# A compact tile for the diagonal blocks of chunked linear attention, and an entry stage that scales by a diagonal product

## The chip, the cores and the metric

The kernel runs on one core of a Trainium2 chip. The metric is the time of one execution in device microseconds, the median of three runs. A core has five engines with a queue of instructions each: TensorE (PE; its weight loads are listed as PEld), VectorE (DVE), ScalarE (ACT), GpSimd (POOL) and SyncE (SP, which here only issues DMAs). An instruction starts when it is at the head of its engine's queue and the semaphores that it waits for are set.

## What is computed

One layer of an encoder on x of 1024 tokens by 1024 channels: a norm, three token mixers side by side (HGRN2, GLA, a gated delta rule), gates, an output product, and a squared-ReLU MLP. The change touches the first norm and the two mixers that are gated linear attention:

```python
h = rmsnorm(x, ln_mix_pre)            # x * rsqrt(mean(x^2) + eps) * w
# gated_linear_attention, per head; f = exp(log_f) per token and key channel
# S_t = diag(f_t) S_{t-1} + k_t v_t^T ;  o_t = S_t^T q_t
# within a chunk: a[i, j] = sum_k q[i, k] * prod_{j < m <= i} f[m, k] * k[j, k]   (j <= i)
# o = a @ v + (q decayed) @ S
```

HGRN2 has 8 heads with values of 128 channels, GLA 4 heads with 256: 12 heads in all.

## The kernel before

A tile scheduler sets the order of the instructions on each engine from a written order of parts (`ORDER`, near line 930), from priorities (`high_priority` with an offset moves instructions ahead) and from its own estimate of durations. The large projections of the normed input with the weights (`product`, line 195; each weight and each activation is split into a high and a low part, and three products are summed) are by far the most of PE's work. The scheduler puts such products between the small matmuls of the mixers, so that PE has something to do while another engine prepares the next small step.

**The entry stage** (`stage_in`): x comes in eight tiles of 128 tokens by 1024 channels, four buffers, two at a time. `front` squares a tile on ACT with a sum, takes the root (`rstd`: a Sqrt on ACT and small DVE steps) and multiplies the tile by it on DVE (line 292). `back` transposes it in blocks of 128 by 128 on PE (line 302, the second operand is the identity) into PSUM banks of four blocks; from there ACT writes the high part `hT_hi` (line 305) and DVE the low part `hT_lo` (line 306). The first projection (`first_project`) follows pair by pair. Two small Exp calls on ACT belong to other parts: line 262 in `lower_bound` and line 380 in `small_part`. Exp and Sqrt lie in different function tables of ACT, and a change of table is an instruction of its own (ACT_TABLE_LOAD).

**Linear attention** (`linear_attention`, one call a head): the 1024 tokens are 8 chunks of 128. The matrix `at` of a chunk (128 keys on the partitions by 128 queries) is built by doubling: at level h, pairs of neighbouring blocks of h tokens are joined, the second half of the queries against the first half of the keys, with q, k already multiplied by the decay inside their blocks. `update(h)` does the multiplying on DVE: q (line 568), k (line 569) and the block decay f (line 570). Up to blocks of 32 the matmuls are of 32 by 32 quadrants: for each chunk c and each quadrant start s in 0, 32, 64, 96 one small product, lines 576 (level 0, bank `E`), 599 (levels 1 and 2 together, bank `L12`, two banks of four chunks) and 611 (h = 4, 8, 16). `put` copies the entries that a level owns from PSUM into `at` with a mask (COPY_PREDICATED, line 561), once for each quadrant s, since in `at` the four quadrants of a chunk lie in different columns. Levels 32 and 64 are plain copies on ACT into `at` (lines 620 and 625, after the matmuls of lines 617 and 624). Then k is transposed (line 631), the state products (line 640) and the attention products that read `at` (line 643) run, and the state is carried from chunk to chunk on DVE (line 649). `at` is cleared at the start by a memset on POOL (line 549).

In a level's sequence each engine waits for the other: the matmuls of the next level read the q and k that `update` has just written, and `update` may not write before the matmuls of its own level have read.

Of the kernel before, what the change touches and what calls it, by code (L numbers as in the profile page):

```python
# [18 lines left out]
P = 128  # L19
# [43 lines left out]
def layout(inputs):  # L63
# [21 lines left out]
    for n, h in enumerate(LEVELS[2:]):  # L85
# [22 lines left out]
        "conv": np.ascontiguousarray(f["gdn_conv"][0].reshape(4, 24, P).transpose(2, 1, 0)),  # L108
        "alog": rows(f["gdn_a_log"][0]),
        "dtb": rows(f["gdn_dt_bias"][0]),  # L110
        "masks": masks,
        "consts": consts,
    }

# [117 lines left out]
def load_consts(p):  # L232
    nc, c, a = p.nc, p.const, p.a
    cs = c.tile([P, 5, P], F32, name="cs")
    nc.sync.dma_start(cs, a["consts"])
    p.ident, p.tri, p.neg, p.ones = (cs[:, i, :] for i in range(4))
    p.fold = cs[:, 4, 0:64]
    p.lnpre = c.tile([P, 8], F32, name="lnpre")
    nc.sync.dma_start(p.lnpre, a["lnpre"])


def load_more(p):
    nc, c, a = p.nc, p.const, p.a
    mk = c.tile([P, 6, 64], F32, name="mk")
    nc.sync.dma_start(mk, a["masks"])
    p.masks = mk.bitcast(I32)
    for n, w in (("onorm", 512), ("lbl", 8), ("bgk", 4), ("alog", 8), ("dtb", 8)):
        t = c.tile([P, w], F32, name=n)
        nc.sync.dma_start(t, a[n])
        setattr(p, n, t)  # L250
    p.conv = c.tile([P, 24, 4], F32, name="conv")
    nc.sync.dma_start(p.conv, a["conv"])
    nc.vector.tensor_scalar(p.onorm, p.onorm, 0.5, None, ALU.mult)


def lower_bound(p):
# [5 lines left out]
    nc.scalar.activation(e, e, AF.Exp)  # L262
    v.reciprocal(mx, e)
    v.tensor_tensor(e, e, mx, ALU.mult)
    v.tensor_tensor(lb, e, e, ALU.subtract)
    v.tensor_scalar(lb, lb, 0.0, 1.0, ALU.max, ALU.min)
    v.tensor_scalar(om, lb, -1.0, 1.0, ALU.mult, ALU.add)
    p.lb, p.om = lb, om


def stage_in(p):

    nc, v = p.nc, p.nc.vector
    hi = p.hp.tile([P, NK, T], F32R, name="hT_hi", tag="hi")
    lo = p.hp.tile([P, NK, T], F32R, name="hT_lo", tag="lo")
    p.h = (hi, lo)

    def front(t):
        xs = []
        for j in range(2):  # L280
            xt = p.stage.tile([P, D], F32, name=p.name("x_in"), tag="x_in", bufs=4)
            with p.tc.high_priority(offset=p.ahead + 100 if t == 0 else 0):
                nc.sync.dma_start(xt, p.a["x"][(t + j) * P:(t + j + 1) * P, :])
            xs.append(xt)
        if t == 0:
            with p.tc.high_priority(offset=p.ahead + 100):
                load_consts(p)
        for xt in xs:
            junk, ms = p.stage.tile([P, D], F32, name=p.name("junk"), tag="junk"), p.tiny("ms_x", 1)
            nc.scalar.activation(junk, xt, AF.Square, scale=D ** -0.5, accum_out=ms)  # L290
            r = p.rstd(ms, p.eps)
            v.tensor_scalar(xt, xt, r, None, ALU.mult)
        return xs

    def back(t, xs):
        dst = slice(t * P, (t + 2) * P)
        for k0 in range(0, NK, 2):
            b = p.bank("xT")
            for i in range(2):
                for j in range(2):  # L300
                    o = (2 * i + j) * P
                    nc.tensor.transpose(b[:, o:o + P], xs[j][:, (k0 + i) * P:(k0 + i + 1) * P], p.ident)
            for i in range(2):
                k, s = k0 + i, b[:, 2 * i * P:2 * (i + 1) * P]
                nc.scalar.activation(hi[:, k, dst], s, AF.Identity, scale=p.lnpre[:, k:k + 1])  # L305
# [25 lines left out]
def bc(ap, shape):  # L331
    return ap.broadcast_to(list(shape))


def small_part(p):
# [41 lines left out]
    la = p.tiny("la", 64)  # L377
    u, t1 = p.tiny("sp_u", 64), p.tiny("sp_t", 64)
    ea = p.tiny("ea", 8)
    act.activation(ea, p.alog, AF.Exp)  # L380
    u3 = u.rearrange("p (h c) -> p h c", h=8)
    v.tensor_tensor(u3, cab[:, :, 0, :].rearrange("p c h -> p h c"), bc(p.dtb.unsqueeze(2), [P, 8, 8]), ALU.add)
    act.activation(t1, u, AF.Abs)
# [158 lines left out]
def linear_attention(p, q, qx, k, f, v_at, dv, o_out, ss_out):  # L542
# [8 lines left out]
    k3 = k.rearrange("p (c i) -> p c i", c=8)  # L551
    q3 = q.rearrange("p (c i) -> p c i", c=8)

    def put(lev, h, data, c=slice(0, 8)):
        dst = at.rearrange("p (c n two h) -> p c n two h", c=8, two=2, h=h)
        dst = dst[:, c, :, 0 if lev == 0 else 1, :]
        w = 16 // h
        for s in range(0, P, 32):
            n, e = slice(s // 32 * w, s // 32 * w + w), slice(s // 2, s // 2 + 16)
            mask = p.masks[s:s + 32, lev, e].rearrange("p (n h) -> p n h", h=h).unsqueeze(1)  # L560
            v.copy_predicated(dst[s:s + 32, :, n, :], bc(mask, [32, c.stop - c.start, w, h]),
                              data[s:s + 32, :, e].rearrange("p c (n h) -> p c n h", h=h))

    def update(h):
        fb, qb, kb = blocks(f, h), blocks(q, h), blocks(k, h)
# [6 lines left out]
    b = p.bank("E").rearrange("p (c i) -> p c i", c=8)  # L572
    quads = range(0, P, 32)
    for c in range(8):
        for s in quads:
            mm(b[s:s + 32, c, s // 2:s // 2 + 16], k3[:, c, s:s + 32], q3[:, c, s:s + 32:2], start=True, stop=True)
    e = b
# [12 lines left out]
    put(0, 1, e[:, :, 0:64])  # L590
    pairs = []
    for c0 in (0, 4):
        b = p.bank("L12").rearrange("p (c i) -> p c i", c=4)
        for j in range(4):
            c = c0 + j
            q2c = qx[:, c * P:(c + 1) * P].rearrange("p (s i) -> p s i", s=2)
            b2 = b[:, j, :].rearrange("p (s i) -> p s i", s=2)
            for s in quads:
                mm(b2[s:s + 32, :, s // 2:s // 2 + 16], k3[:, c, s:s + 32], q2c[:, :, s // 2:s // 2 + 16], start=True, stop=True)
        pairs.append((b, slice(c0, c0 + 4)))  # L600
    update(2)
    for b, c in pairs:
        put(1, 1, b[:, :, 0:64], c)
        put(2, 2, b[:, :, 64:128], c)
    for lev, h in ((3, 4), (4, 8), (5, 16)):
        b = p.bank("L").rearrange("p (c i) -> p c i", c=8)
        qb = q.rearrange("p (c n two h) -> p c n two h", c=8, two=2, h=h)
        for c in range(8):
            for s in quads:
                n = slice(s // (2 * h), (s + 32) // (2 * h))  # L610
                mm(b[s:s + 32, c, s // 2:s // 2 + 16], k3[:, c, s:s + 32], qb[:, c, n, 1, :], start=True, stop=True)
        update(h)
        put(lev, h, b[:, :, 0:64])
    b = p.bank("L32").rearrange("p (c i) -> p c i", c=8)
    for c in range(8):
        for s in (0, 64):
# [956 lines left out]
```

## Time and profile before

| | us |
|---|---|
| median of 3 runs (2445.07 to 2454.31) | 2445.74 |
| the profiled execution, its own time | 2446.99 |
| its span in the trace | 2445.2 |
| PE busy | 2366.8 |
| DVE busy | 1477.2 |
| ACT busy | 929.1 |
| POOL busy | 86.0 |

A row of the page or of the trace names the engine, the line, the operation and the tiles it writes and reads ("out<-in"), the shape, and in brackets how long the engine stood idle before it and what ended the wait. Matmuls are pipelined: the time beside a matmul is from its start to its modelled end, and the next one starts sooner. In an fp32 product each matmul of the program is recorded as two instructions.

### The profile page before, as it was taken

To read this page: it belongs to the slowest core of one execution; us is meant where nothing else is said; L and a number is where in the kernel's file an instruction comes from. 1 tells how busy PE (TensorE), PEld (TensorE's weight loads), DVE (VectorE), ACT (ScalarE), POOL (GpSimd) and SP (SyncE) were. 2 spreads that over 40 slices of the span, in tenths; PEclk is the share of its full clock that TensorE was granted. 3 is DMA by queue.
4 is the path that set the end of the run, shared out by engine and by line. 5 is a ranking of instruction groups with operands and counts; after the bars stand their busy time and mean duration, and the time that the engine had idled before them with its cause. 6 is when DMAs were issued, how large, how long until landed. Compare 5 with 4: busy or idle time off the path is not lost. (4 is left out here: it accounts for less than half of the span.)

```text
span 2445.2 us, 46222 instructions
## 1 busy us (share of the span) xinstructions
PE 2366.8 (97%) x18782; PEld 2060.4 (84%) x18782; DVE 1477.2 (60%) x3187; ACT 929.1 (38%) x1920; POOL 86.0 (4%) x160
## 2 busy tenths in 40 slices
PE   7999989999999999999999999999999999999998
PEld 6778878988977988889898889998877888788886
DVE  5284599955655446654446654445658655557577
ACT  6863424132323222222221332232434655544453
POOL 0000000000000000000000000000001211100000
PEclk9999999999999999999999999999999999999999
DMA  4455612142221222112221202233333444575454
GB/s 146 138 188 148 192 54 95 36 152 71 66 66 36 72 85 66 49 36 74 87 74 54 70 28 80 57 109 115 115 124 113 168 143 142 181 228 187 153 160 155
DMA packets 166071, 263.64 MB, mean 108 GB/s; under 512 B 42833, under 2 KB 80977, under 8 KB 165729
## 3 DMA queue, kind: packets, MB, share of 16 engines
q1 hardware_dynamic: 145248, 208.23, 27.6%
q0 software_dynamic: 10240, 33.56, 3.8%
q10 hardware_dynamic: 10368, 18.88, 2.1%
q8 instruction: 148, 2.42, 0.4%
q14 instruction: 67, 0.54, 0.1%
HBM read 190.29 MB, written 70.32 MB: 107 GB/s over the span
## 5 line engine op out<-in xcount | busy, mean ns | idle before, releaser
L195 PE MATMUL pj<-whi,hT_hi 128*128 128x256 f32 (+1 forms) x2048 | 581.1, 284 | 6.1 <-ACT hT_hi L305 5.7
L195 PE MATMUL pj<-whi,hT_lo 128*128 128x256 f32 (+1 forms) x2048 | 580.5, 284 | 0.0
L195 PE MATMUL pj<-wlo,hT_hi 128*128 128x256 f32 (+1 forms) x2048 | 579.7, 283 | 0.0
L195 PEld LDWEIGHTS pj<-whi,hT_hi 128*128 128x128 f32 x2048 | 388.2, 190 | 8.6 <-ACT hT_hi L305 6.5
L195 PEld LDWEIGHTS pj<-wlo,hT_hi 128*128 128x128 f32 x2048 | 387.9, 190 | 1.0
L195 PEld LDWEIGHTS pj<-whi,hT_lo 128*128 128x128 f32 x2048 | 387.0, 189 | 1.3 <-issue 0.4
L195 PE MATMUL pj<-hT_hi,whi 128*128 128x512 f32 x768 | 310.7, 405 | 0.0
L195 PE MATMUL pj<-hT_hi,wlo 128*128 128x512 f32 x768 | 309.7, 403 | 0.0
L195 PE MATMUL pj<-hT_lo,whi 128*128 128x512 f32 x768 | 307.7, 401 | 0.0
L168 DVE TENSOR_TENSOR wlo<-wraw,whi 128x1024 fp32r<-128x1024 f32 (+2 forms) x122 | 147.8, 1212 | 158.5 <-ACT whi L168 118.0
L168 ACT CAST whi<-wraw 128x1024 fp32r<-128x1024 f32 (+2 forms) x122 | 126.7, 1039 | 168.9 <-DMA wraw<-in_w_dram 107.2
L195 PE MATMUL ps<-whi,whi 128*128 128x512 f32 x448 | 175.1, 391 | 2.6 <-ACT whi L168 2.4
L195 PE MATMUL ps<-wlo,whi 128*128 128x512 f32 x448 | 175.1, 391 | 0.4 <-DVE wlo L168 0.4
L195 PEld LDWEIGHTS pj<-hT_hi,wlo 128*128 128x128 f32 x768 | 146.0, 190 | 34.5 <-issue 2.3
L195 PE MATMUL ps<-whi,wlo 128*128 128x512 f32 x448 | 175.0, 391 | 0.0
L195 PEld LDWEIGHTS pj<-hT_lo,whi 128*128 128x128 f32 x768 | 145.7, 190 | 32.4 <-issue 1.5
L195 PEld LDWEIGHTS pj<-hT_hi,whi 128*128 128x128 f32 x768 | 146.0, 190 | 31.6 <-issue 0.9
L897 ACT ACTIVATE gs<-pj 128x256 f32<-128x256 f32 x96 | 36.8, 384 | 320.4 <-PE pj L195 312.2
L900 DVE SCALAR_TENSOR_TENSOR gt<-gs 128x256 f32<-128x256 f32 x96 | 40.4, 424 | 160.4 <-ACT gs L898 157.3
L195 PE MATMUL ps<-h_hi,whi 128*128 128x512 f32 x272 | 108.1, 398 | 3.3 <-ACT whi L168 3.3
L195 PE MATMUL ps<-h_hi,wlo 128*128 128x512 f32 x272 | 108.1, 397 | 1.1 <-DVE wlo L168 1.1
L195 PE MATMUL ps<-h_lo,whi 128*128 128x512 f32 x272 | 108.0, 397 | 0.0
(383 smaller groups left out, 4073.9 us busy)
## 6 DMA issues: line engine op xcount, KB each, us to landing
wraw<-in_w_dram SPq DMA_DIRECT2D x110, 512.0 KB, 3.9
uin<-ud SPq DMA_DIRECT2D x112, 256.0 KB, 2.7
ud<-us POOLq DMA_DIRECT2D x64, 256.0 KB, 2.8
uraw<-in_wup_dram SPq DMA_DIRECT2D x60, 256.0 KB, 3.7
b<-in_wdown_dram SPq DMA_DIRECT2D x48, 256.0 KB, 3.6
ud<-q POOLq DMA_DIRECT2D x26, 256.0 KB, 2.3
x_in<-in_x_dram SPq DMA_DIRECT2D x8, 512.0 KB, 5.5
browb<-brow SPq DMA_DIRECT2D x16, 256.0 KB, 5.3
```

Source lines behind the costliest of these rows:

```text
L168: return self.nc.scalar.copy(hi, raw), self.nc.vector.tensor_tensor(lo, raw, hi, ALU.subtract)
L195: self.nc.tensor.matmul(bank, x, y, start=first and not (opened or more), stop=last and close, skip_group_check=more)
L897: act.activation(sg[:, :, 0:128], b[:, :, 0:128], AF.Silu)
L900: v.scalar_tensor_tensor(gt, sg[:, :, 128:256], 1.0, sg[:, :, 0:128], ALU.add, ALU.mult)
```

## The change

1. **Compact tile.** `put` no longer writes into `at`. A tile `dg` of 128 partitions by 8 chunks by 32 columns takes the diagonal 32 by 32 blocks: quadrant s lies on partitions s to s+31, and all four share the same 32 columns. The matmuls write their banks in the same shape, so one masked copy on 128 partitions does for a level what four did. Levels 1 and 2 share one bank instead of two, and have one copy each. The masks are cut to 16 columns on the host. `dg` is cleared by a memset on POOL, and four POOL copies put its quadrants into `at` after the last of these levels.
2. **Diagonal product.** `front` no longer multiplies x; it multiplies the 128 by 128 identity by the scale, and `back` uses a full matmul of x with that diagonal instead of the transpose.
3. **Held-back Exp.** The two Exp calls are issued after the last `hT_hi` of the entry stage.
4. **Loads of x.** All x loads have a raised priority, not the first pair alone.

```diff
-        "masks": masks,
+        "masks": np.stack([masks[j:j + 32, :, j // 2:j // 2 + 16] for j in range(0, P, 32)]).reshape(P, 6, 16),
...
+    with p.tc.issue_after(p.last_hi.ins):
+        nc.scalar.activation(e, e, AF.Exp)
...
-            with p.tc.high_priority(offset=p.ahead + 100 if t == 0 else 0):
+            with p.tc.high_priority(offset=p.ahead + 100 if t == 0 else p.ahead):
...
-            v.tensor_scalar(xt, xt, r, None, ALU.mult)
+            d = p.m("x_scale")[:, :P]
+            v.tensor_scalar(d, p.ident, r, None, ALU.mult)
+            out.append((xt, d))
...
-                    nc.tensor.transpose(b[:, o:o + P], xs[j][:, (k0 + i) * P:(k0 + i + 1) * P], p.ident)
+                    x, d = xs[j]
+                    nc.tensor.matmul(b[:, o:o + P], x[:, (k0 + i) * P:(k0 + i + 1) * P], d, start=True, stop=True)
...
-    act.activation(ea, p.alog, AF.Exp)
+    with p.tc.issue_after(p.last_hi.ins):
+        act.activation(ea, p.alog, AF.Exp)
...
+    dg = p.m("diag")[:, :256]
+    nc.gpsimd.memset(dg, 0.0)
+
+    def put(lev, h, data):
+        dst = dg.rearrange("p (c n two h) -> p c n two h", c=8, two=2, h=h)[:, :, :, 0 if lev == 0 else 1, :]
+        mask = p.masks[:, lev, :].rearrange("p (n h) -> p n h", h=h).unsqueeze(1)
+        v.copy_predicated(dst, bc(mask, [P, 8, 16 // h, h]), data.rearrange("p c (n h) -> p c n h", h=h))
...
+    b = p.bank("L12")[:, :256].rearrange("p (c two i) -> p c two i", c=8, two=2)
...
-                mm(b[s:s + 32, c, s // 2:s // 2 + 16], k3[:, c, s:s + 32], qb[:, c, n, 1, :], start=True, stop=True)
+                mm(b[s:s + 32, c, :], k3[:, c, s:s + 32], qb[:, c, n, 1, :], start=True, stop=True)
         update(h)
-        put(lev, h, b[:, :, 0:64])
+        put(lev, h, b)
+    for s in quads:
+        nc.gpsimd.tensor_copy(at3[s:s + 32, :, s:s + 32], dg[s:s + 32, :].rearrange("p (c i) -> p c i", c=8))
```

The scheduler makes a new order of it. On DVE, in the eighth head (the sixth of HGRN2), from the copy of q into `qx` to the update of k at h = 4; `wlo` is the low part of a weight split, `mk` the masks, `E` and `L` the banks of the levels. Before:

```order
L588 COPY qx_10413<-q_10412 128x8x64
L168 TENSOR_TENSOR wlo_11335<-wraw_11332,whi_11334 128x1024
L561 COPY_PREDICATED at_10990<-mk,E_10992 32x8x16 x4
L568 TENSOR_TENSOR q_10412<-q_10412,f_10415 128x256x2
L569 TENSOR_TENSOR k_10414<-k_10414,f_10415 128x256x2
L561 COPY_PREDICATED at_10990<-mk,L_1459_11035 32x4x16
L570 TENSOR_TENSOR f_10415<-f_10415 128x256
L561 COPY_PREDICATED at_10990<-mk,L_1459_11035 32x4x16 x3
L561 COPY_PREDICATED at_10990<-mk,L_1459_11035 32x4x8x2 x4
L561 COPY_PREDICATED at_10990<-mk,L_1460_11052 32x4x16 x4
L561 COPY_PREDICATED at_10990<-mk,L_1460_11052 32x4x8x2 x4
L568 TENSOR_TENSOR q_10412<-q_10412,f_10415 128x128x4
L569 TENSOR_TENSOR k_10414<-k_10414,f_10415 128x128x4
```

And in the changed kernel, the same stretch:

```order
L593 COPY qx_10274<-q_10273 128x8x64
L168 TENSOR_TENSOR wlo_11175<-wraw_11172,whi_11174 128x1024
L568 COPY_PREDICATED diag_10853<-mk,E_10855 128x128
L574 TENSOR_TENSOR q_10273<-q_10273,f_10276 128x256x2
L575 TENSOR_TENSOR k_10275<-k_10275,f_10276 128x256x2
L568 COPY_PREDICATED diag_10853<-mk,L_1468_10895 128x128
L576 TENSOR_TENSOR f_10276<-f_10276 128x256
L568 COPY_PREDICATED diag_10853<-mk,L_1468_10895 128x64x2
L574 TENSOR_TENSOR q_10273<-q_10273,f_10276 128x128x4
L575 TENSOR_TENSOR k_10275<-k_10275,f_10276 128x128x4
```

Between the two updates of k stood 16 masked copies; now there are 2. On PE the 512-wide filling products of this head stood 10, 17, 7 and 7 ahead of the matmuls of h = 4, 8, 16 and of blocks of 32; now they are 7, 7, 7 and 7. Heads 5 to 12 have 4 to 9 of them ahead of h = 4 (5 to 10 before) and 7 ahead of the rest (17 before at h = 8). In heads 1 to 4 DVE has other work between the levels of the changed kernel: weight splits, the subtraction at line 425, steps of the solver (lines 531 and 533), and the small steps of a reciprocal root.

On ACT, in the entry stage, around the first Exp (`lb_e`); `junk` is the squaring of an x tile, `rq_y` the root. Before:

```order
L305 ACTIVATE hT_hi<-xT_345,lnpre 128x256
L262 ACT_TABLE_LOAD
L262 ACTIVATE lb_e<-lb_e 128x8
L290 ACTIVATE junk_314,ms_x_315<-x_in_299 128x1024
L168 CAST whi_165<-wraw_163 128x1024
L223 ACT_TABLE_LOAD
L223 ACTIVATE rq_y_317<-ms_x_315,eps 128x1
L305 ACTIVATE hT_hi<-xT_327,lnpre 128x256
```

And where both Exp calls stand in the changed kernel:

```order
L311 ACTIVATE hT_hi<-xT_564,lnpre 128x256
L168 CAST whi_961<-wraw_959 128x1024
L311 ACTIVATE hT_hi<-xT_573,lnpre 128x256 x2
L387 ACT_TABLE_LOAD
L387 ACTIVATE ea_676<-alog 128x8
L755 COPY v_491<-pj_582 128x256
L263 ACTIVATE lb_e<-lb_e 128x8
```

The two switches of table within the entry stage, and the one ahead of the second Exp, have become one, behind the last `hT_hi`.

## Rows read from the trace of the kernel before

**Rows 1.** The page, part 1: busy us (share of the span), instructions, by engine.

```profile
PE 2366.8 (97%) x18782; PEld 2060.4 (84%) x18782; DVE 1477.2 (60%) x3187; ACT 929.1 (38%) x1920; POOL 86.0 (4%) x160
```

**Rows 2.** Waits of PE: line waited for: us in total, times, longest us.

```profile
PE L L611 <- DVE k L569: 38.2, 32, 2.3
...
PE pj L195 <- ACT hT_hi L305: 5.7, 2, 3.8
...
PE L L617 <- DVE k L569: 1.1, 5, 0.3
```

**Rows 3.** Timeline of the eighth head: start us, us, instructions [idle before <-releaser].

```profile
1008.78 0.76 PE L599 MATMUL L<-qx,k 128*32 128x32 f32 x64
...
1010.70 1.78 DVE L561 COPY_PREDICATED at<-mk,E 32x128 f32<-32x128 int32 x4
...
1013.86 0.74 PE L611 MATMUL L<-q,k 128*32 128x16 f32 x64 [1.80 <-DVE k L569]
...
1014.63 4.75 DVE L561 COPY_PREDICATED at<-mk,L 32x64 f32<-32x64 int32 x15
...
1020.84 0.73 PE L611 MATMUL L<-q,k 128*32 128x16 f32 x64 [2.11 <-DVE k L569]
...
1022.28 0.69 DVE L568 TENSOR_TENSOR q<-q,f 128x512 f32<-128x512 f32 x1
...
1022.89 0.69 DVE L569 TENSOR_TENSOR k<-k,f 128x512 f32<-128x512 f32 x1
...
1022.99 0.40 PE L195 MATMUL pj<-hT_hi,wlo 128*128 128x512 f32 x1
...
1023.73 0.73 PE L611 MATMUL L<-q,k 128*32 128x16 f32 x64 [0.34 <-DVE k L569]
```

**Rows 4.** Instructions of line 561: count, duration ns min/median/max, first and last start, forms.

```profile
L561 DVE COPY_PREDICATED at<-mk,L x336: 283/294/315, 127.6 to 1449.2; 32x64 f32<-32x64 int32 x96, 32x128 f32<-32x128 int32 x72
L561 DVE COPY_PREDICATED at<-mk,E x48: 422/441/458, 120.5 to 1432.1; 32x128 f32<-32x128 int32 x48
```

**Rows 5.** The page, part 5: weight splits on DVE: busy us, mean ns | idle before.

```profile
L168 DVE TENSOR_TENSOR wlo<-wraw,whi 128x1024 fp32r<-128x1024 f32 (+2 forms) x122 | 147.8, 1212 | 158.5 <-ACT whi L168 118.0
```

**Rows 6.** Timeline of the entry stage, ACT and PE.

```profile
22.66 1.28 ACT L262 ACT_TABLE_LOAD   x1
...
26.15 1.28 ACT L223 ACT_TABLE_LOAD   x1
...
27.45 0.29 ACT L223 ACTIVATE rq_y<-ms_x,eps 128x1 f32<-128x1 f32 x1
...
28.16 0.61 PE L195 MATMUL pj<-whi,hT_hi 128*128 128x288 f32 x1 [3.80 <-ACT hT_hi L305]
...
38.18 1.28 ACT L380 ACT_TABLE_LOAD   x1
...
40.10 0.49 PE L195 MATMUL pj<-whi,hT_hi 128*128 128x288 f32 x1 [1.92 <-ACT hT_hi L305]
```

**Rows 7.** Windows: us, busy of PE, PEld, DVE, ACT, POOL, granted clock, DMA share, GB/s.

```profile
28.00:32.00 4.00, 3.85 (x16) 3.66 (x17) 3.92 (x11) 2.79 (x8) 0.00 (x0) 0.50 0.29 96
40.00:44.00 4.00, 3.90 (x18) 3.89 (x19) 2.44 (x6) 2.23 (x7) 0.00 (x0) 0.57 0.00 0
1080.00:1084.00 4.00, 3.44 (x71) 2.73 (x71) 3.83 (x11) 0.00 (x0) 0.00 (x0) 0.67 0.02 4
```

**Rows 8.** Timeline of PE: transposes of the entry stage, and fp32 products (line 467).

```profile
36.70 1.47 PE L302 MATMUL xT<-cs,x_in 128*128 128x128 f32 x12
...
166.62 1.95 PE L467 MATMUL kk<-ks 128*128 128x128 f32 x16
...
168.32 0.48 PE L195 MATMUL pj<-hT_lo,whi 128*128 128x512 f32 x1
```

**Rows 9.** Groups on POOL: memsets, by shape: busy us, mean ns | idle before.

```profile
L549 POOL MEMSET at<- 128x1024 f32 x12 | 11.5, 959 | 914.2 <-PE pj L195 620.2 <-DVE wlo L168 119.3 <-issue 61.3
...
L804 POOL MEMSET z<- 64x256 f32 x16 | 4.9, 307 | 683.5 <-DVE gt L905 188.3 <-issue 101.3 <-DMA xs<-xt 95.8
```

More of the change, by code (lines that the diff above doesn't have):

```diff
@@ L243, in load_more @@
     nc, c, a = p.nc, p.const, p.a
-    mk = c.tile([P, 6, 64], F32, name="mk")
+    mk = c.tile([P, 6, 16], F32, name="mk")
     nc.sync.dma_start(mk, a["masks"])
@@ L261, in lower_bound @@
     v.tensor_tensor(e, p.lbl, mx, ALU.subtract)
-    nc.scalar.activation(e, e, AF.Exp)
+    with p.tc.issue_after(p.last_hi.ins):
+        nc.scalar.activation(e, e, AF.Exp)
     v.reciprocal(mx, e)
@@ L287, in front @@
                 load_consts(p)
+        out = []
         for xt in xs:
@@ L291, in front @@
             r = p.rstd(ms, p.eps)
-            v.tensor_scalar(xt, xt, r, None, ALU.mult)
-        return xs
+            d = p.m("x_scale")[:, :P]
+            v.tensor_scalar(d, p.ident, r, None, ALU.mult)
+            out.append((xt, d))
+        return out
     def back(t, xs):
@@ L301, in back @@
                     o = (2 * i + j) * P
-                    nc.tensor.transpose(b[:, o:o + P], xs[j][:, (k0 + i) * P:(k0 + i + 1) * P], p.ident)
+                    x, d = xs[j]
+                    nc.tensor.matmul(b[:, o:o + P], x[:, (k0 + i) * P:(k0 + i + 1) * P], d, start=True, stop=True)
             for i in range(2):
                 k, s = k0 + i, b[:, 2 * i * P:2 * (i + 1) * P]
-                nc.scalar.activation(hi[:, k, dst], s, AF.Identity, scale=p.lnpre[:, k:k + 1])
+                p.last_hi = nc.scalar.activation(hi[:, k, dst], s, AF.Identity, scale=p.lnpre[:, k:k + 1])
                 v.scalar_tensor_tensor(lo[:, k, dst], s, p.lnpre[:, k:k + 1], hi[:, k, dst], ALU.mult, ALU.subtract)
@@ L552, in linear_attention @@
     q3 = q.rearrange("p (c i) -> p c i", c=8)
[L554 to L562, printed above, removed]
+    dg = p.m("diag")[:, :256]
[4 more added lines that the diff above has]
+        v.copy_predicated(dst, bc(mask, [P, 8, 16 // h, h]), data.rearrange("p c (n h) -> p c n h", h=h))
     def update(h):
@@ L570, in update @@
         v.tensor_tensor(second, second, first, ALU.mult)
-    b = p.bank("E").rearrange("p (c i) -> p c i", c=8)
+    e = p.bank("E")[:, :128].rearrange("p (c i) -> p c i", c=8)
     quads = range(0, P, 32)
@@ L575, in linear_attention @@
         for s in quads:
-            mm(b[s:s + 32, c, s // 2:s // 2 + 16], k3[:, c, s:s + 32], q3[:, c, s:s + 32:2], start=True, stop=True)
-    e = b
+            mm(e[s:s + 32, c, :], k3[:, c, s:s + 32], q3[:, c, s:s + 32:2], start=True, stop=True)
     f2, q2, k2 = blocks(f, 1), blocks(q, 1), blocks(k, 1)
@@ L589, in linear_attention @@
              q.rearrange("p (c n two h) -> p c n two h", c=8, two=2, h=2)[:, :, :, 1, :])
[L590 to L600, printed above, removed]
+    put(0, 1, e)
+    b = p.bank("L12")[:, :256].rearrange("p (c two i) -> p c two i", c=8, two=2)
+    for c in range(8):
+        q2c = qx[:, c * P:(c + 1) * P].rearrange("p (s i) -> p s i", s=2)
+        for s in quads:
+            mm(b[s:s + 32, c, :, :], k3[:, c, s:s + 32], q2c[:, :, s // 2:s // 2 + 16], start=True, stop=True)
     update(2)
-    for b, c in pairs:
-        put(1, 1, b[:, :, 0:64], c)
-        put(2, 2, b[:, :, 64:128], c)
+    put(1, 1, b[:, :, 0, :])
+    put(2, 2, b[:, :, 1, :])
     for lev, h in ((3, 4), (4, 8), (5, 16)):
-        b = p.bank("L").rearrange("p (c i) -> p c i", c=8)
+        b = p.bank("L")[:, :128].rearrange("p (c i) -> p c i", c=8)
         qb = q.rearrange("p (c n two h) -> p c n two h", c=8, two=2, h=h)
@@ L610, in linear_attention @@
                 n = slice(s // (2 * h), (s + 32) // (2 * h))
-                mm(b[s:s + 32, c, s // 2:s // 2 + 16], k3[:, c, s:s + 32], qb[:, c, n, 1, :], start=True, stop=True)
+                mm(b[s:s + 32, c, :], k3[:, c, s:s + 32], qb[:, c, n, 1, :], start=True, stop=True)
         update(h)
-        put(lev, h, b[:, :, 0:64])
+        put(lev, h, b)
+    for s in quads:
+        nc.gpsimd.tensor_copy(at3[s:s + 32, :, s:s + 32], dg[s:s + 32, :].rearrange("p (c i) -> p c i", c=8))
     b = p.bank("L32").rearrange("p (c i) -> p c i", c=8)
```

## The prediction

> **What bounds the kernel now.** I read the page's busy line first. TensorE (PE) is busy 2366.8 of 2445.2 us, VectorE (DVE) 1477.2 [rows 1]: PE sets the end nearly everywhere, so what DVE saves counts only where PE stands still for DVE, and the whole of PE's idle time, 78 us, is the most that removing waits could give. The list of waits, kept to PE, says where that idle time lies: 38.2 us in 32 waits on one edge, the level matmuls (line 611) behind the update of k on DVE (line 569), and 1.1 us on its continuation at line 617; 5.7 us in the entry stage, products behind ACT's `hT_hi` [rows 2]. Nothing else on that list is of that size.
>
> Next I read one of the 12 heads of linear attention, the eighth, on PE and DVE together [rows 3]. Between two levels PE runs products of a projection that the scheduler put there as filling; then it stops until DVE has updated q and k. After the matmuls at 1013.86 come 17 filling products, and PE still waits 2.11 us at 1020.84. DVE is never idle in that time: 15 masked copies take 4.75 us from 1014.63 on, and the next updates of q and k queue behind them. After 1020.84 come 7 products and a wait of 0.34. Before 1013.86 four masked copies (1.78 us) stand in the same place and PE waits 1.80. So the masked copies are on the path: late copies, late update, late PE.
>
> **What the change does to DVE.** Before, a head has 4 copies for level 0, 16 for levels 1 and 2, and 12 for the last three: 32. After, 6. What does one of them cost when it covers 128 partitions? No row shows that. The rows give two sizes on 32 partitions, 0.294 us at 64 or 128 elements in a partition and 0.441 us for 128 elements in runs of one [rows 4]: doubling the elements moved nothing there, so I take 0.29 to 0.44 us, as one of the old ones. The other end is that it costs as much as the four it replaces, 1.2 to 1.8 us; it is the slow rival below. DVE loses 26 copies a head, some 8 us, 96 us in all; I count none of that but the part under PE's waits.
>
> **What PE waits for afterwards.** PE's side of a step: from the start of level matmuls to the end of the seventh product 2.55 us (1020.84 to 1022.99 and 0.40), and 0.23 us for each product more (17 of them: 1013.86 to 1018.73, where the wait of 2.11 begins) [rows 3]. DVE's side: level matmuls 0.73, then q to k 0.61 (1022.28 to 1022.89), k to the next PE start 0.84 (to 1023.73) [rows 3]: with a hand-over of 0.05, 2.23 us. The scheduler has changed its filling too: between the last levels it still puts 7 products, where it put 17 it now mostly puts 7, and ahead of the first of these levels 4 to 9 instead of 5 to 10.
> - Steps from h=8 on: one copy and the f update hide under the 0.73 us of matmuls; 2.23 is under 2.55, no wait.
> - The step of levels 1 and 2: f and the first copy take 0.77 us (1013.86 to 1014.63 [rows 3]), the second copy at most 0.44, then 0.61 + 0.84: 2.66 against 2.55, a wait of 0.1; 1 us over heads 5 to 12.
> - The step before it: matmuls 0.76, then 0.05 + 0.61 + 0.84, 2.26. With 7 products no wait; with only 4 (1.86 us) 0.4, in four heads, 1.6 us. In five heads a weight split of 1.21 us [rows 5] stands on DVE ahead of or between the updates, and PE waits 0.5: 2.5 us. In two (the eighth and eleventh) the split itself starts late: the copies began 1.92 us after the matmuls (1008.78 to 1010.70 [rows 3]), so 1.92 + 0.44 + 1.45 is 3.81 against 2.55: 1.3 each, 2.5 us.
> - Heads 1 to 4 now carry other DVE work between the levels (splits, pieces of the solver, a reciprocal root). I price these at 1.2 us a head, one split, though no row sizes their mix: 4.8 us; ends 0 and 10.
> This leaves 12 us of 39: **27 us gained** (ends 20 and 36).
>
> **Clock.** In the stretch 1080 to 1084 the granted clock is 0.67, between the two levels 1.2 and 2.4 GHz, after a wait of the 2 us kind [rows 7]. That is 1.3 us of work (0.33 of 4 us); one such window stands in the rows, and the windows near 320, 1328 and 1440, in the second, tenth and twelfth head, are like it. If the waits shrink to tenths, these drops should go: **4 us gained** (0 to 7).
>
> **Entry stage.** Three edits. The scale is put into a 128 by 128 diagonal, and a true fp32 product with it replaces the transpose. Twelve transposes take 1.47 us with the last one's 0.27 us tail, 0.11 each [rows 8]; eight fp32 products of the same shape (recorded as 16) take from 166.62 to 168.32, 0.21 each [rows 8]. PE gains 64 x 0.10 = 6.6 us of work, and some 1.2 us more for the first dozen, before the clock is up. Against it stand two Exp calls that are now held back until the last `hT_hi`. Before, the first brings a table load at 22.66 and another at 26.15 to go back to the root; the second loads at 38.18; behind them `hT_hi` is late, and PE stands 3.80 us before 28.16 and 1.92 before 40.10 [rows 6]. Then it runs at a clock of 0.50 (28 to 32) and 0.57 (40 to 44) [rows 7]: 3.7 us more. Without the loads and with x loaded no later, both gaps should close: 9.4 gained, 7.8 paid, **2 us gained** (ends: 6 lost, 8 gained). What would be late next is the third piece of the first weights, whose load stands behind an x load that waits for these slower products to release a buffer: about 1 us, within the ends.
>
> The rows show a table load of 1.28 us, and the next activation starts at 27.45, 0.02 us behind its end [rows 6]. The Trainium skill, "ScalarE: Activation LUTs", section "What ACT_TABLE_LOAD costs", puts a switch at 2.66 us with a drain of about 1.38; this trace has no room for the drain, and by the page's figure the entry stage would gain 3 us more, 2410.
>
> **Costs that I put at nothing.** On POOL a head gets one more memset and four copies from the compact tile into `at`. Nothing of POOL of that kind ran before; the nearest row is a memset of 64 x 256 at 0.307 us [rows 9]. The attention product that reads `at` comes two levels, the transposes of k and the state products after the last masked copy: two steps of 2.55 us at least [rows 3]. Four copies at 0.31 to 1.2 us each fit. The memset of the compact tile stands on POOL ahead of the first copy, where the old one of 0.96 us stood [rows 9]. The smaller mask load and the single bank for levels 1 and 2 are off the path.
>
> **Sum.** 27 + 4 + 2 = 33 us. The profiled execution took 2446.99 us (span 2445.2), 1.25 over the median of 2445.74; 33 less than the median is **2413 us**.
>
> **Rivals.**
> - *POOL holds DVE up* (chance 0.13). While POOL reads the compact tile, q and k updates on DVE wait. In the steps after the last masked copy PE has 0.32 us to spare in each of two (2.55 less 2.23). Four copies at 0.307 [rows 9] in line with DVE cost 1.23 - 0.64 = 0.6 us a head, 7 us; at twice that length 1.8 a head, 22 us: 2420 to 2435. For it: DVE has no gap there; against it: copies are short and matmuls of a level give room. The Trainium skill, "SBUF — State Buffer", section "Who interferes with whom", says that a DVE instruction with two SBUF inputs contends with a GpSimd instruction that reads SBUF, one blocking the other for its whole length; that speaks for this rival, and no row of before has POOL reading.
> - *A masked copy on 128 partitions costs as four* (0.03; the slow side). DVE's chain is then what it was, but the filling is not: from 17 products to 7, the step of levels 1 and 2 leaves PE standing 10 x 0.23 = 2.3 us longer, 28 us over 12 heads, and nothing is won: 2446 + 28 = 2474. It decides against the change from a copy of about 1 us on.
> - *The gain comes back elsewhere* (0.06): PE gets ahead of DVE's solver or of loads, and new waits of 20 us and more stand in other places: 2440. Against it: PE hardly waits for either now.
> - *Entry at its bad end* (0.08): the gaps stay and the products are paid: 2413 + 8 = 2421.
> - *All ends good* (0.10): 36 + 7 + 8 = 51 us, 2395.
>
> **How the numbers follow.** The forecast has 0.60 (2402 to 2424 by its own ends). With the good end, POOL's hold-up and the entry's bad end that is 0.91; the rest is wait returned or slower. The range is 2396 to 2434. Half a per cent, about what a measurement here can tell from no change, is 12 us: faster needs less than 2433.5. Faster 0.89, same 0.07, slower 0.04.
>
> **What would show it.** Right: the wait of the level matmuls for k falls from 38 to some 10 us, masked copies are 72 at 0.3 to 0.45 us, no clock drop at 1080 to 1450, one table load at about 50 us, PE busy a few us more in the first 60. Wrong: masked copies at over 1 us; attention products waiting for POOL; q or k updates longer than 0.69 us beside POOL copies; gaps at 20 to 45 us that stay.

## The result, and the profile after

The changed kernel takes 2406.39 us (median of 4 runs, 2401.18 to 2408.47); the kernel before, on the same chip, 2447.35. The ratio is 0.9825 (95% interval 0.9806 to 0.9845): 41 us faster, where 33 were forecast. The profiled execution took 2404.39 us with a span of 2402.6, 42.6 under the span of before.

The page, part 1, of the changed kernel (busy us, share of the span, instructions), beside [rows 1]:

```profile
PE 2366.7 (99%) x18846; PEld 2063.8 (86%) x18846; DVE 1375.5 (57%) x2875; ACT 925.5 (39%) x1916; POOL 119.7 (5%) x220
```

PE is as busy as it was (2366.8); its idle time fell from 78 to 36 us. DVE lost 101.7 us, and only the part of it that stood under PE's waits was worth anything. The list of PE's waits (us in total, times, longest), beside [rows 2]:

```profile
PE xT L308 <- DVE x_scale L296: 7.6, 2, 7.1
PE ps L195 <- ACT whi L168: 6.2, 3, 2.4
PE L L610 <- DVE k L575: 2.6, 5, 1.3
PE L L610 <- issue: 1.6, 5, 0.5
...
PE kT L632 <- DVE k L575: 0.2, 1, 0.2
```

The level matmuls waited 39.3 us for k in 37 places (lines 611 and 617; 0.8 us in 4 more at line 624); 2.6 us in 5 are left, 4.4 with the 0.2 on k's transposes and the 1.6 that the profile puts down to the instruction's own issue. The waits for `hT_hi` are gone from the list. The eighth head, PE and DVE (start us, us, instructions [idle before <-releaser]), beside [rows 3]:

```profile
990.00 0.76 PE L600 MATMUL L<-qx,k 128*32 128x32 f32 x64
...
990.08 1.23 DVE L168 TENSOR_TENSOR wlo<-wraw,whi 128x1024 fp32r<-128x1024 f32 x1 [0.36 <-ACT whi L168]
991.22 0.44 DVE L568 COPY_PREDICATED diag<-mk,E 128x128 f32<-128x128 int32 x1
...
992.69 0.45 DVE L568 COPY_PREDICATED diag<-mk,L 128x128 f32<-128x128 int32 x1
...
992.83 0.74 PE L610 MATMUL L<-q,k 128*32 128x16 f32 x64 [0.25 <-DVE k L575]
...
993.47 0.44 DVE L568 COPY_PREDICATED diag<-mk,L 128x128 f32<-128x128 int32 x1
...
995.33 0.74 PE L610 MATMUL L<-q,k 128*32 128x16 f32 x64
...
1001.09 0.69 DVE L574 TENSOR_TENSOR q<-q,f 128x512 f32<-128x512 f32 x1 [0.82 <-PE L L618]
1001.70 0.89 DVE L575 TENSOR_TENSOR k<-k,f 128x512 f32<-128x512 f32 x1
```

From the matmuls of levels 1 and 2 to those of h = 8 it took 12.06 us before (1008.78 to 1020.84) and now takes 5.33; of the 6.7 us between them 3.7 are PE's waits, and 3.0 are 13 filling products that now stand elsewhere. Where 16 masked copies stood between the two updates of k there are two, and from the next step on DVE waits for PE. One thing is new: the last update of k shown takes 0.89 us, and POOL is copying out of the compact tile at that moment.

The masked copies of the changed kernel and its POOL copies (count, ns min/median/max, first and last start), beside [rows 4]:

```profile
L568 DVE COPY_PREDICATED diag<-mk,L x60: 268/295/465, 132.6 to 1409.0; 128x128 f32<-128x128 int32 x60
L568 DVE COPY_PREDICATED diag<-mk,E x12: 434/437/451, 124.5 to 1397.9; 128x128 f32<-128x128 int32 x12
L614 POOL COPY at<-diag x48: 387/760/1235, 140.1 to 1411.2; 32x256 f32<-32x256 f32 x48
```

Windows of the changed kernel (us, busy of PE, PEld, DVE, ACT, POOL, granted clock, DMA share, GB/s), beside [rows 7]:

```profile
28.00:32.00 4.00, 4.00 (x32) 4.00 (x31) 3.35 (x12) 3.97 (x9) 0.00 (x0) 1.00 0.93 326
...
60.00:64.00 4.00, 4.00 (x9) 2.46 (x8) 0.00 (x0) 4.00 (x9) 0.00 (x0) 0.50 0.00 0
72.00:76.00 4.00, 4.00 (x7) 1.66 (x6) 0.00 (x0) 2.14 (x5) 0.00 (x0) 0.50 0.00 0
...
1080.00:1084.00 4.00, 4.00 (x23) 3.42 (x22) 0.87 (x1) 0.97 (x2) 0.00 (x0) 1.00 0.64 184
```

A copy on 128 partitions costs what one on 32 did. The stretch at 28 us now has a clock of 1.00 where it had 0.50, and 1080 has 1.00 where it had 0.67. But at 60 to 80 us PE runs at 1.2 GHz, half its clock, although it is busy all the time. The times at which four places are reached show where each part of the 42.6 us came from (us from the span's start; `smT` is the first transpose of the decay part, `cum` its last step, E and L64 the first and the last level matmuls of the heads):

| stretch | before | after | difference |
|---|---|---|---|
| start to smT (entry stage) | 58.2 | 52.8 | -5.4 |
| smT to cum (decay part) | 23.1 | 30.9 | +7.8 |
| cum to the first E | 36.9 | 36.9 | 0 |
| first E to the last L64 (twelve heads) | 1332.8 | 1291.4 | -41.4 |
| last L64 to the end | 994.2 | 990.6 | -3.6 |

So the heads gave nearly all. The last stretch is no part of the change; it takes 988 to 995 us in the 14 traces at hand. The entry stage gave 5.4 us, and the decay part behind it lost 7.8, a stretch that the change does not touch and that the prediction did not name. Was that a price of the change?

### The profile page after: what moved, and what is told of

Same layout as the page of the kernel before. It is cut to its first block, busy times and chain, and to the rows that moved or that the text cites. A ratio compares the mean times of both kernels' runs of the same rounds, so it can differ in the third digit from the quotient of the medians.

```text
span 2402.6 us, 46134 instructions
## 1 busy us (share of the span) xinstructions
PE 2366.7 (99%) x18846; PEld 2063.8 (86%) x18846; DVE 1375.5 (57%) x2875; ACT 925.5 (39%) x1916; POOL 119.7 (5%) x220
```

## Experiments

Theory at the start: the heads hold the whole gain, because the number of masked copies between two updates of k is what PE waited for; the entry's gain is real, but by coming to the decay part sooner it is lost to the clock there. Rivals: the entry's gain lasts; the gain in the heads comes from the shared bank or the new order; POOL's copies take something back. The kernels ran in three sets on three chips, each set with its own runs of the kernel before (medians 2446.98, 2451.26 and 2449.93), so ratios to it are compared across sets and microseconds within one.

### Each part alone

Compact tile alone, the entry stage as before:

```
-    with p.tc.issue_after(p.last_hi.ins):
-        nc.scalar.activation(e, e, AF.Exp)
+    nc.scalar.activation(e, e, AF.Exp)
...
-                    nc.tensor.matmul(b[:, o:o + P], x[:, ...], d, start=True, stop=True)
+                    nc.tensor.transpose(b[:, o:o + P], x[:, ...], p.ident)
```

> The compact tile alone: the entry stage is that of the kernel before (transposes, x scaled, both Exp calls where they were, x loads as before). Theory: the twelve heads hold the whole gain and what the new entry wins by 53 us is lost again by 84 us to the half clock, so this kernel takes as long as the changed one: 39 to 43 us less than before, 2404 to 2408; smT at 58 us, the fp32 products of 16 rows (line 363 of the changed kernel) at full clock but for some 4 us as before, cum at 81 us. Rival: the entry's gain lasts, and without it some 5 us of the 41 are missing: 2411 to 2413.

Measured: 2404.24 us (2396.46 to 2408.74, 5 runs), ratio 0.9821 (0.9797 to 0.9844), the same as the whole change. The heads take 1292.0 us in its trace, against 1332.8 and 1291.4. But the clock was not as expected. Windows of this kernel:

```profile
60.00:64.00 4.00, 4.00 (x8) 1.99 (x7) 0.09 (x1) 3.96 (x9) 0.00 (x0) 0.50 0.00 0
72.00:76.00 4.00, 4.00 (x7) 1.66 (x6) 0.00 (x0) 2.14 (x4) 0.00 (x0) 0.50 0.00 0
76.00:80.00 4.00, 4.00 (x7) 1.55 (x7) 0.00 (x0) 1.71 (x4) 0.00 (x0) 0.50 0.00 0
80.00:84.00 4.00, 4.00 (x7) 2.10 (x8) 0.00 (x0) 2.13 (x5) 0.00 (x0) 0.50 0.00 0
```

With the old entry stage the decay part ran at half clock for longer still, 34.0 us from smT to cum. So it is not the new entry that brings it: the theory's second half falls, and the time within its range is no support for it.

The entry edits alone, heads as before (the same edits, the other way round):

> The entry edits alone (diagonal product, held-back Exp, priority of the x loads), heads as in the kernel before. Theory (gain taken back by the clock): smT at 53 us instead of 58, then half clock for some 20 us between 56 and 81 us, cum at 83 to 84 us, and 2444 to 2450 in all, no difference from before. Rival (the gain lasts): cum at 76 us, 5 us less, 2440 to 2442. The waits of the level matmuls for k stay at 38 us by both.

Measured: 2449.86 us (2443.51 to 2455.74, 12 runs), ratio 1.0011 (0.9997 to 1.0026). Its trace has smT at 53.79 and cum at 83.12, and the list of waits has the heads as they were:

```profile
PE L L618 <- DVE k L576: 37.0, 30, 2.3
```

The two runs agree with each other: the heads are worth the whole, the entry nothing that can be measured while the decay part takes anything from 23 to 34 us.

### What takes the clock away in the decay part

The decay product there (line 363 of the changed kernel) is an fp32 matmul over 16 rows. The edit pads both operands with zeros to 128 rows, and leaves order, columns and results alone:

```
-    wgk = p.m("wgk")[0:16, :512]
+    wgk = p.m("wgk")[:, :512]
+    nc.gpsimd.memset(wgk, 0.0)
...
-        s = p.m("sm")[0:16, :512]
-        act.copy(s, b[0:16, :])
+        s = p.m("sm")[:, :512]
+        nc.gpsimd.memset(s, 0.0)
+        act.copy(s[0:16, :], b[0:16, :])
```

> The changed kernel with the two operands of the decay product (line 363: 16 rows, fp32) padded with zeros to 128 rows; the same products in the same order, the same columns, nothing else changed. Theory A (the stretch falls to 1.2 GHz because so few rows of the array work): no half clock between 54 and 84 us, pairs at 1.12 us throughout, cum at 75 to 77 us, 2398 to 2400. Theory B (rows do not matter; it is the fp32 products with their slow weight loads, or the phase): half clock stays for 15 to 22 us, cum at 83 to 84 us, 2405 to 2407.

Measured: 2395.3 us (2393.96 to 2400.91, 5 runs), ratio 0.9795 (0.9771 to 0.9818). One pair of the products in the changed kernel, at half clock (timeline of PE):

```profile
73.01 2.07 PE L363 MATMUL fb<-sm,wgk 16*128 16x512 f32 x2
```

One pair in the kernel before, at full clock, with the two products behind it:

```profile
66.68 1.12 PE L357 MATMUL fb<-sm,wgk 16*128 16x512 f32 x2
67.73 0.50 PE L195 MATMUL pj<-hT_lo,whi 128*128 128x512 f32 x1
68.07 0.39 PE L195 MATMUL pj<-hT_hi,wlo 128*128 128x512 f32 x1
```

The same in the padded kernel:

```profile
65.02 1.02 PE L365 MATMUL fb<-sm,wgk 128*128 128x512 f32 x2
65.48 0.79 PE L195 MATMUL pj<-hT_lo,whi 128*128 128x512 f32 x1
66.11 0.40 PE L195 MATMUL pj<-hT_hi,wlo 128*128 128x512 f32 x1
```

And windows of the padded kernel:

```profile
60.00:64.00 4.00, 4.00 (x16) 2.42 (x14) 0.00 (x0) 4.00 (x8) 0.00 (x0) 1.00 0.00 0
72.00:76.00 4.00, 3.12 (x15) 2.52 (x16) 0.45 (x2) 3.94 (x5) 0.00 (x0) 1.00 0.00 0
```

The clock stays at 1.00 up to 1700 us, smT to cum takes 20.8 us, and PE is early enough to stand for 1.1 us in front of cum. That puts cum at 72.9 us and the whole at 2395.3, both below what theory A expected. The rows were the one thing changed in the program, so it is the products of 16 rows that bring the fall to 1.2 GHz, among them or just behind them, while the profile shows PE busy without a gap: the clock falls there in all five traces without the padding and in none of the nine with it. What it is about these products is not settled. Even at full clock a pair and the product behind it take 1.39 us with 16 rows (66.68 to 68.07) and 1.09 padded (65.02 to 66.11), and the ends of matmuls are modelled, so PE may stand in part of the 16-row pairs; the rows that are filled and such pauses were not told apart. Padded, the changed kernel has the ratio 0.979 to 0.980, and the other padded versions with few masked copies further down lie between 0.978 and 0.984.

The same padding in the kernel before:

> The kernel before with the two operands of the decay product padded with zeros to 128 rows, the same order on every engine. Theory (the half clock behind the 16-row products comes in every kernel, for a length that differs from run to run, and is what scatters the runs of before over 2441 to 2455): no half clock at 56 to 92 us, the runs within 6 us of each other, and a median of 2438 to 2442. Rival (only the new entry brings the long stretch): before loses no more than its 4 us, 2444 to 2447, with the scatter it has.

Measured: 2443.51 us (2440.89 to 2447.67, 5 runs), ratio 0.9963 (0.9950 to 0.9977). smT to cum takes 20.7 us, with a clock of 1.00. The median misses the expected range by 1.5 us. The trace is of the slowest of the five (2447.67 us): summed over windows of 8 us, the clock that is missing in its heads comes to 13.5 us of work, where the profile of before has 6.7, and in the entry stage to 3.4.

The kernel before paid for the 16 rows too. The mean granted clock of its nine executions on this chip is 0.988, of the five padded ones 0.991, and 0.003 of 2445 us is some 7 us, as much as the medians differ (7.8). For the changed kernel it is 0.9925 in four executions and 0.996 padded, some 8 us. So the padding gives both kernels about the same, and the +7.8 us of the table are no price of the change. The traces without the padding have one execution each, and the stretch takes 23 to 34 us in them (before 23.1, entry alone 29.3, after 30.9, heads alone 34.0, transposes kept 34.0). Multiplied by the granted clock of the stretch (0.93, 0.71, 0.67, 0.60, 0.60) these come to 20.4 to 21.5 us, where the padded kernels take 20.7 to 21.0: the clock is nearly the whole difference. That it goes by the execution, and not only by the kernel, the kernel with transposes shows, whose six executions lie between 2412.63 us at a clock of 0.989 (the one profiled) and 2390.35 at 0.997, the clock of padded kernels.

### What the entry edits are worth

With the padding the rest can be weighed. The changed kernel once more, and the compact tile alone, both padded, in the same set:

> The changed kernel with the padded decay product once more, as the measure for the other three on the same chip: 2394 to 2398, smT at 52 to 53 us, no half clock before 1700 us. Against the kernel before with the same padding theory says 41 to 45 us less (twelve heads 41, entry 0 to 5).

> The compact tile alone, with the padded decay product. With the clock out of the way the entry edits can be weighed: theory (they are worth the 5 us seen at smT, 58.2 before and 52.8 after): 2399 to 2402, that is 4 to 6 us over the changed kernel with the same padding. Rival (they are worth nothing, as the run of the entry alone has it): within 2 us of it, 2394 to 2397.

Measured: 2401.17 us (2396.01 to 2402.38) and 2402.61 us (2398.09 to 2404.55), ratios 0.9789 (0.9775 to 0.9802) and 0.9796 (0.9783 to 0.9809). Against the padded kernel before that is 42.3 us, where 41 to 45 were expected (in absolute time it lies 3 us over its range), and 40.9. In whole times the entry edits come to 1.4 us, nearer to the rival, and inside the scatter of 6; the theory's 4 to 6 are neither shown nor excluded by them. The traces show more. When the x tiles come differs from run to run (the third group of transposes or products starts at 13.8 to 16.7 us), so the measure is from that group to smT:

| kernels | third group to smT, us |
|---|---|
| before; padded | 43.1; 42.3 |
| compact tile alone; padded | 41.0; 41.6 |
| product, Exp not held back (padded) | 41.0 |
| transposes, Exp held back; padded | 40.2; 40.3 |
| whole entry: after; six other runs | 38.5; 38.3 to 38.7 |

Undoing the diagonal product:

```
-            d = p.m("x_scale")[:, :P]
-            v.tensor_scalar(d, p.ident, r, None, ALU.mult)
-            out.append((xt, d))
+            v.tensor_scalar(xt, xt, r, None, ALU.mult)
+            out.append((xt, None))
...
-                    nc.tensor.matmul(b[:, o:o + P], x[:, ...], d, start=True, stop=True)
+                    nc.tensor.transpose(b[:, o:o + P], x[:, ...], p.ident)
```

> The changed kernel with the diagonal product undone (x scaled on DVE, transposed on PE), Exp still held back and x loads still early. Theory (the closed gaps come from the held-back Exp; the product only adds work to PE): smT at 46 to 49 us instead of 53, by the 6.6 us of work saved; in all 2400 to 2408, the lower end if the clock then stays up, the upper if half clock takes it back. Rival (the scaling of 128 by 1024 on DVE is what held the transposes up): the gaps ahead of hT_hi reopen, smT at 55 us or later, 2408 to 2412.

> The changed kernel with transposes for the diagonal product (Exp held back, x loads early) and the padded decay product. Theory (the 6.6 us of work saved on PE come back as waits for x and hT_hi, as smT at 55.3 us in the run of it says): 2395 to 2399, no better than the diagonal product with the same padding. Rival (that profile was an unlucky one; the shortest run of this entry was 2390): smT at 50 us or earlier, 2388 to 2392.

Measured: 2396.58 us (2390.35 to 2412.63, 6 runs), ratio 0.9801 (0.9773 to 0.9829); padded 2399.79 us (2396.04 to 2400.22), ratio 0.9784 (0.9770 to 0.9797), the same as with the product. smT comes at 55.26 and 54.08 us, not at the theory's 46 to 49; the gaps reopen, as the rival had it, yet the median of the first is under the ranges of both. The 6.6 us of PE work that transposes save are not gained: PE arrives early and stands. PE in the unpadded one (timeline):

```profile
32.92 0.40 PE L195 MATMUL pj<-whi,hT_hi 128*128 128x288 f32 x1 [1.15 <-ACT hT_hi L310]
33.91 0.40 PE L195 MATMUL pj<-whi,hT_hi 128*128 128x288 f32 x1 [0.46 <-DVE narrow L755]
...
35.96 0.61 PE L195 MATMUL pj<-whi,hT_hi 128*128 128x288 f32 x1 [0.81 <-ACT hT_hi L310]
```

Behind these gaps its clock is 0.50 from 36 to 40 us. Scaling a 128 by 1024 tile holds DVE for 0.75 us, scaling the diagonal for 0.29. That this is what the stage loses was only argued; ahead of the first gap `hT_hi` stands on ACT behind a cast of weights that waited for its load:

```profile
31.45 1.04 ACT L168 CAST whi<-wraw 128x1024 fp32r<-128x1024 f32 x1 [1.09 <-DMA wraw<-in_w_dram]
32.40 0.47 ACT L310 ACTIVATE hT_hi<-xT,lnpre 128x256 fp32r<-128x256 f32 x1
```

Letting the two Exp calls go where they were:

```
-    with p.tc.issue_after(p.last_hi.ins):
-        act.activation(ea, p.alog, AF.Exp)
+    act.activation(ea, p.alog, AF.Exp)
```

> The changed kernel with the padded decay product, the two Exp calls no longer held back (diagonal product and early x loads kept). Theory (it is the held-back Exp that closes the gaps ahead of hT_hi): two more table loads between 18 and 45 us, waits of PE for hT_hi of 3 to 6 us and a clock drop behind them, smT at 56 to 59 us instead of 52 to 54, and 3 to 6 us over the same kernel with Exp held back (2395 to 2401 in its two calls). Rival (the early x loads alone close the gaps): smT at 52 to 54 us and the same time.

Measured: 2403.47 us (2398.98 to 2405.29, 5 runs), ratio 0.9812 (0.9796 to 0.9828). The held-back version had 0.9789 and 0.9795, with intervals that overlap with it, so the whole times do not tell the two apart. The table loads are back (timeline of ACT):

```profile
21.12 1.28 ACT L262 ACT_TABLE_LOAD   x1
...
24.05 1.28 ACT L223 ACT_TABLE_LOAD   x1
...
36.65 1.28 ACT L387 ACT_TABLE_LOAD   x1
```

PE waits 1.9 us for `hT_hi`, under the 3 to 6 expected, its clock does not drop, and smT comes at 55.5, just under the 56 to 59 expected. The stage is 2.5 us longer. So with the rest of the entry edits in place, holding Exp back is worth about 2.5 us and the product some 1.7. Each without the other gives less by the table (about 1 us, and 0.6 at most, against the compact tile alone), and all together give 2.5 to 3 us there and 4 to 5 against the kernel before. The early x loads were not undone by themselves.

### Is it the number of masked copies?

```
-        v.copy_predicated(dst, bc(mask, [P, 8, 16 // h, h]), data...)
+        for s in range(0, P, 32):
+            v.copy_predicated(dst[s:s + 32], bc(mask[s:s + 32], [32, 8, 16 // h, h]), data[s:s + 32]...)
```

> The changed kernel with the padded decay product, each masked copy split into four of 32 partitions (24 a head instead of 6), compact tile and single bank kept; the scheduler puts 10 and 12 products ahead of h = 4 and h = 8 where it had 7 and 7. Theory (the number of masked copies between two updates of k is what PE waits for): copies of 0.29 us, DVE busy about 60 us more, waits of the level matmuls for k of 18 to 28 us with the longest 0.8 to 1.5, a few drops of the clock behind them: 2415 to 2430. Rival (the gain came from the shared bank or the new order, not from the count): waits under 8 us, 2395 to 2404.

Measured: 2442.07 us (2438.93 to 2446.46, 11 runs), ratio 0.9973 (0.9961 to 0.9985), within a few us of the padded kernel before (0.9963). Everything is lost, more than expected. Its waits of PE:

```profile
PE L L613 <- DVE k L578: 33.0, 28, 2.4
```

Its eighth head, DVE and PE:

```profile
1011.77 3.23 DVE L571 COPY_PREDICATED diag<-mk,L 32x128 f32<-32x128 int32 x7
...
1016.45 0.73 PE L613 MATMUL L<-q,k 128*32 128x16 f32 x64 [1.89 <-DVE k L578]
```

24 copies a head cost as much as 32 did, and two things go with that. DVE is busy 1463.3 us, 88 more than with 6 copies and only 14 less than before, where some 60 more were expected: the copies of levels 1 and 2 now hold 128 elements in runs of one and two and take 0.44 us, not 0.29, which is some 14 of the 28. And the scheduler puts 12 products ahead of h = 8 where 17 stood, so less of DVE's work has cover. The clock drops in the heads are back too (11.8 us lost). Shared bank, tile, order of the levels and entry stage are those of the changed kernel: the count of copies, with the DVE time that goes with it, is the gain.

### POOL and DVE on the same tiles

Every copy three times:

```
+        for _ in range(3):
             nc.gpsimd.tensor_copy(at3[s:s + 32, :, s:s + 32], dg[s:s + 32, :]...)
```

> The changed kernel with the padded decay product, each of the four copies on POOL issued three times (same order on PE and DVE). From the last copy to the attention product that reads at there were 4.9 to 5 us in ten of twelve heads; a quarter set takes 2.55 us. Theory A (POOL gives way to DVE; only PE's wait for at can cost): the 5.1 us more just fill the margin, q and k updates stay near 0.68 us, waits of PE for at of 0.1 to 0.5 us in most heads and up to 10 us in the third head, where DVE works without a break: 2 to 12 us more than without, 2399 to 2412. Theory B (the forecast's rival: DVE stands while POOL reads): q and k updates beside the copies at 0.9 us and more, 4 to 6 updates a head longer by 0.2 to 0.8, waits of the level matmuls for k of 10 us and more: 2410 to 2425.

And the four copies on ACT:

```
-        nc.gpsimd.tensor_copy(at3[s:s + 32, :, s:s + 32], dg[s:s + 32, :]...)
+        act.copy(at3[s:s + 32, :, s:s + 32], dg[s:s + 32, :]...)
```

> The changed kernel with the padded decay product, the four copies out of the compact tile on ACT instead of POOL (five rows of PE's order and a few of DVE's differ). If POOL and DVE hinder each other at a price: no q or k update over 0.70 us, no wait of PE for at (1.6 us in one run), 2 to 4 us less than with POOL. If they do not: the same time within 2 us. ACT takes 0.35 to 0.40 us a copy, some 1.5 us a head, beside 60 per cent idle time.

Measured: three times, 2411.32 us (2406.41 to 2412.84), ratio 0.9842 (0.9826 to 0.9858); on ACT, 2398.11 us (2394.04 to 2398.92), ratio 0.9789 (0.9774 to 0.9804). The q updates with the copies on ACT (count, ns min/median/max, first and last start):

```profile
L576 DVE TENSOR_TENSOR q<-q,f x72: 677/692/753, 124.1 to 1406.0; 128x512 f32<-128x512 f32 x72
```

The same in the padded changed kernel:

```profile
L576 DVE TENSOR_TENSOR q<-q,f x72: 674/692/914, 121.9 to 1408.7; 128x512 f32<-128x512 f32 x72
```

PE's waits with three times the copies:

```profile
PE o L647 <- POOL at L617: 5.6, 4, 2.1
PE kT L635 <- DVE k L577: 3.1, 6, 0.8
```

Both theories of the tripled run hold in part. Of 144 updates of q and k, 48 take 0.73 us or more, 23 with the copies done once, 6 with them on ACT; their excess over 0.69 sums to 6.7, 3.0 and 0.3 us. PE waits for both: 5.6 us for `at` and 3.1 for k. ACT waits too, 53.9 us in 8 places, where it writes the next blocks into `at`; what that holds up was not separated from the rest of the 13 us. As the kernel stands, 3 us of DVE's time are lost and PE sees next to none of it: on ACT the ratio is the same, within the 3 to 4 us that the interval allows.

Who gives way is not always DVE. In the third head of the padded changed kernel, where DVE runs solver steps and updates without a break (timeline of POOL):

```profile
347.20 9.34 POOL L616 COPY at<-diag 32x256 f32<-32x256 f32 x4 [21.64 <-DVE f L578]
```

DVE in the same stretch:

```profile
348.09 0.68 DVE L576 TENSOR_TENSOR q<-q,f 128x512 f32<-128x512 f32 x1
348.70 0.68 DVE L577 TENSOR_TENSOR k<-k,f 128x512 f32<-128x512 f32 x1
```

And PE's wait for it, in the list of waits:

```profile
PE o L646 <- POOL at L616: 1.6, 1, 1.6
```

Here DVE keeps its 0.68 us and four POOL copies take 9.34 instead of 2.55, so that PE waits 1.6 us for `at`. In the profile of the changed kernel the same four took 3.48 us and the updates beside them 0.90 and 0.88.

## Why the prediction was right, step by step

**What bounds the kernel, and where it waits: right.** The waits for k were on the path, and the 24-copy kernel brings them back together with the whole time.

**Cost of a copy: right.** Forecast 0.29 to 0.44 us on 128 partitions; measured 0.295 and 0.437. The rival with copies as dear as four falls.

**Waits left: too many, 12 forecast, 4.4 measured; 35 us gained instead of 27.** The steps from h = 8 on have none for k in heads 5 to 12, as forecast. The term that was most off is that of heads 1 to 4: 4.8 us for other DVE work between the levels, 0.9 measured; the splits and solver steps stand where DVE has time. In the step of the late split the forecast let the first copy start 1.92 us after the matmuls, as before; in the eighth head the split now starts 0.08 us after them and the copy at 1.22, so the wait is 0.25 instead of 1.3. In the eleventh it is 1.26, as forecast. The remaining small steps were put at 5.1 us and came to some 2.

**Clock in the heads: right in kind, low in size.** All four drops between 320 and 1450 us are gone, 6.7 us where 4 were forecast (ends 0 and 7). 35 and 6.7 come to 41.7; the heads took 41.4 us less. That is this pair of executions, and the profile of before is one with few drops: the three other traces with the waits for k have 7 or 8 in the heads (11.8 and 13.5 us were given above), those with few masked copies none to two. So the term is undersized, and in other executions lies beyond its upper end.

**Entry: right in sign; the working was wrong in one place.** 2 us were forecast, as 9.4 gained less 7.8 paid for the products (ends 6 lost, 8 gained). By the second table it was 2.5 to 5 us, by the kernel that it is measured against. The products do take 0.21 us each, and PE is 5.3 us busier between 16 and 52 us; but the stage is no shorter with transposes, since PE then waits for `hT_hi`, so that work is not paid in full. The step left out of the reading two waits of the entry's size in the list of before, 9.7 us for x and 5.7 for weights at line 168; the change left them much as they were (7.6 and 6.2). The Trainium skill, "ScalarE: Activation LUTs", section "What ACT_TABLE_LOAD costs", puts a table switch at 2.66 us with a drain of about 1.38, by which the stage was to gain 3 us more. The trace agrees on the load, 1.28 us, but not on the drain: in the run with the two calls let go, the activations ahead of and behind the loads stand 0.01 to 0.02 us from them, and moving three loads out of the way of `hT_hi` was worth 2.5 us in all.

**Not in the forecast: the decay part.** The profile of before showed it, and the rows were not read (windows of before; the clock is the third number from the end):

```profile
72.00:76.00 4.00, 4.00 (x11) 2.40 (x12) 0.00 (x0) 4.00 (x8) 0.00 (x0) 0.80 0.00 0
76.00:80.00 4.00, 4.00 (x15) 3.17 (x14) 0.45 (x2) 3.94 (x6) 0.00 (x0) 0.77 0.01 4
```

It added 7.8 us in the profiled pair (23.1 and 30.9 us). There the heads gave 10 us more than the 31 forecast for them, and the two misses partly cancel: that the total came out as near as it did is in part luck.

**POOL: the rival's mechanism is real, its price is not.** Updates of 0.88 to 0.90 us beside POOL were named as a sign of it, and are there. The forecast gave it 7 to 22 us, with copies one after the other in DVE's way. But an update loses 0.2 us at a time, less than the 0.32 us which the forecast had found to spare in a step, and in heads 5 to 12 only one update a head is slowed: in the eighth head k takes 0.89 us at 1001.70, and the matmuls behind it do not wait. The Trainium skill, "SBUF — State Buffer", section "Who interferes with whom", says that a DVE instruction with two SBUF inputs contends with a GpSimd instruction that reads SBUF, calls the shared pair of ports an exclusive lock, and lets the issue order decide who is blocked. The trace agrees that they slow each other, in either direction: 0.90 instead of 0.69 us on DVE in one place, 9.34 instead of 2.55 us on POOL in another. That an update waits for the whole of a POOL copy the rows do not show: it loses 0.2 us, and the shortest copy takes 0.39.

## What to carry to other kernels

When an engine waits for another, count the instructions between two hand-overs on the other one, and merge those whose cost doesn't grow with partitions; then look at what the scheduler does with the cover, since filling is planned to the work that it hides. Before weighing an edit of a few us, find the stretch that varies most from run to run, and fix or fence it off: padding one product was worth some 8 us here, more than the entry edits gave.

## What the runs showed of the hardware

- PE's clock fell to 1.2 GHz among or just behind fp32 products of 16 rows, with no idle time of PE in the profile; with 128 rows, 112 of them zero, it stayed at 2.4 GHz, 20.8 instead of 23 to 34 us for the stretch.
- At 2.4 GHz a pair of such products with the next product took 1.39 us with 16 rows and 1.09 with 128.
- A masked copy takes 0.29 us for 64 or 128 elements a partition, 0.44 for 128 in runs of one or two, on 32 or 128 partitions alike.
- A POOL copy of 32 by 256 takes 0.39 us at its shortest and 0.76 in the median of the changed kernel; beside DVE work without a break, four of them took 9.34 us in one execution and 3.48 in another, where the DVE updates took 0.88 to 0.90 instead of 0.69.
